# Two more unit pairs a layer by seven quarter products, and the first down operand split before the rest

## The chip, the cores and the metric

The kernel runs on one core of a Trainium2 chip. A core has a matrix engine (TensorE, in the profile PE, with its weight loads as PEld), a vector engine (DVE), a scalar engine (ACT), a general engine (POOL) and a queue that issues DMAs (SP). Matrix products are accumulated in eight PSUM banks; everything else lies in SBUF. The metric is the device time of one execution in microseconds (us), the median of three runs.

## The reference

Two decoder layers over 512 tokens of width 1024, all in float32. A layer has a mixing half (one wide input projection, a gated delta rule and a sliding-window attention, two up-projections, a merge and an output projection) and an MLP half. The change touches the MLP half alone:

```
h2 = rmsnorm(x, pre_mlp_g[l])                              # 512 x 1024
ff = jnp.square(jax.nn.relu(h2 @ w_ff1[l])) @ w_ff2[l]     # 1024 -> 4096 -> 1024
x = x + rmsnorm(ff, post_mlp_g[l])
```

## The kernel before

**Products of split operands.** Every float32 operand is split into a high part (`wh`, `h_h`, `P_h`; a cast by ACT) and a low part (`wl`, `h_l`, `P_l`; a subtraction by DVE). Each product of 128-row blocks is three matmuls: high by high, high by low, low by high.

**Weights.** They come packed in HBM, in pieces of 128 x 1024 float32 (512 KB), loaded by SP into raw buffers `wr` (six of them, `WR = 6`). `prefetch` casts a raw piece to `wh` (line 384, ACT) and subtracts to `wl` (line 385, DVE), into four buffers each (`LOOK = 4`). A call of `weights()` hands out the next prepared piece and prepares up to the third piece after it. So a piece is prepared early only as far as TensorE frees the buffers of the fourth piece before it.

**The MLP half.** The 4096 hidden columns are worked in four blocks, s = 0 to 3, of 1024. A block is an up part (eight units of 128 hidden columns for all 512 tokens) and a down part (1024 hidden columns times 1024 output columns).

- *A plain unit* (`mm_a`, lines 400 to 402) is 24 matmuls with 512 moving columns. Its bank is `ps_f1`, shown as `ps_f` in the profile. ACT takes relu and square from it (lines 1560, 1561 in `done`).
- *A pair of units* (`ff1`) is computed as a 2 x 2 product by seven quarter products in place of eight (Winograd's form). Each is 12 matmuls with 256 moving columns (`mm_h`, lines 473 to 476), so 84 a pair. The sums of activations (`n1` to `n4`) are made once a layer by `combos`, during block 0. The sums of weights are made for each pair by DVE in `up_specs` (line 343: four additions of 128 x 512). They need both raw units of the pair and two more raw buffers. A pair hands out four pieces: the two raw halves (first operand), two sums (second and third), and a half-wide tail (fourth). The intermediate results lie in banks `ps_a` (pool PM), `ps_y` (PZ), `ps_z` (PS) and `ps_q` (PK). The last two quarter products of a pair (`rest`) are issued after the first product of what follows.
- *The down part* of blocks 0 to 2 is also seven products, named after their left operands P1, P5, P6, P2, P7, P3, P4, each 24 matmuls with 512 columns (`mm_c`, lines 461 to 465). The left operands are quarters of the activated block and sums of them. They are made by `lefts` (seven splits and four vector additions, lines 1536 to 1542), once for each four units: `raw[0]` holds units 0 to 3, `raw[1]` holds 4 to 7, and `lefts` is called after the fourth and the eighth unit that is done. The right operands are sums of raw weights, made by DVE (`seven`, lines 304 and 309). Block 3 has a plain down part (`mm_b4`, `last_tiles`), and its activations are split directly (`h3`).
- When the block that follows begins with a pair, the second half of P4 is issued after that pair's first product (`split4`, `fourth`, `pending`).

**Which units are pairs** stands in `SEQ` (line 45), one entry a block: none in block 0; two in block 1, (4,5) and (2,3), between plain units 0, 1 and 6, 7; three in block 2, (0,1), (4,5), (2,3), then plain 6 and 7; four in block 3.

**The order of the work.** The framework fixes each engine's order at build time: earlier in the program has precedence, and an instruction whose inputs are ready can be put ahead of an earlier one that still waits. In `ff1` the order of TensorE is pinned as written (`Order`). On the other engines only the framework's order holds, and once built it is fixed: an instruction that waits holds up those behind it.

Of the kernel before, what the change touches and what calls it, by code (L numbers as in the profile page):

```python
# [41 lines left out]
WR = 6  # L42
FF_ORDER = (0, 4, 1, 5, 2, 6, 3, 7)
XB = 6
SEQ = (FF_ORDER, (0, 1, (4, 5), (2, 3), 6, 7), ((0, 1), (4, 5), (2, 3), 6, 7), ((0, 1), (2, 3), (4, 5), (6, 7)))

MIX = "G K K G K K G K K G K K G GA GA GA".split()
NA = sum(c.count("A") for c in MIX)
# [5 lines left out]
def units(seq):  # L54
    return [m for e in seq for m in (e if isinstance(e, tuple) else (e,))]
# [42 lines left out]
def chunk_keys(depth):  # L98

    keys = {}  # L100
    for kind, *key in chunk_order(depth):
        if kind == "chunk":
            keys[tuple(key)] = None
        elif kind == "up":
            l, s = key
            for m in units(SEQ[s]):
                keys["w_ff1", l, 0, (s * 8 + m) * P, 0] = None
# [20 lines left out]
def hybrid_trunk(ctx, tc, x, positions, pre_mix_g, dn_conv_w, dn_a_log, dn_dt_bias, dn_norm_g,  # L128
# [20 lines left out]
    def pool_of(tag, bufs):  # L149
        def get(name, dt=F32, n=512):  # L150
            return up.tile([P, n], dt, name=name, tag=tag, bufs=bufs)
        return get
# [5 lines left out]
    T = [pool_of(f"t{i}", 4) for i in range(9)]  # L158
# [14 lines left out]
    def PZ(name):  # L173
        return pp.tile([P, 512], F32, name=name, tag="ss", bufs=2)

    def PM(name):
        return pm.tile([P, 512], F32, name=name, tag="pm")
# [144 lines left out]
    def up_specs(l, s):  # L322
# [25 lines left out]
        last = None  # L348
        for n, e in enumerate(SEQ[s]):
            two = isinstance(e, tuple)  # L350
# [12 lines left out]
    for kind_, *key in chunk_order(depth):  # L363
        if kind_ == "seven":
            specs.extend(seven(*key))
        elif kind_ == "up":
            new = up_specs(*key)
            if isinstance(SEQ[key[1]][0], tuple):
                new.insert(1, specs.pop())
# [119 lines left out]
    def pair(U, name):  # L489
        return U(name + "_h", F32R), U(name + "_l", F32R)  # L490
# [104 lines left out]
    for l in range(depth):  # L595
# [859 lines left out]
        def ff1(done, rest=None):  # L1455
# [3 lines left out]
            order.begin()  # L1459
            for n, e in enumerate(SEQ[s]):  # L1460
                if not isinstance(e, tuple):
                    ps = PM("ps_f1")
                    w = weights()
                    if rest is None and not any(isinstance(x, tuple) for x in SEQ[s][n + 1:n + 2]):
                        mm_a(ps, h2, w=w)
# [55 lines left out]
        for s in range(3):  # L1521
            left = {f"P{i}": [] for i in range(1, 8)}
            later = {"P2": [], "P7": [], "P3": []}
            raw = [None, None]

            def make(name, T_, src, sign=1.0):
                p_ = pair(T_, name)
                split(src, *p_, sign)
                left[name].append(p_)

            def lefts(X, Y):

                a11, a21, a12, a22 = X[:, 0:512], X[:, 512:1024], Y[:, 0:512], Y[:, 512:1024]
                make("P1", T[5], a11)
                s1, s2 = T[4]("S1"), T[4]("S2")
                tt(out=s1, in0=a21, in1=a22, op=ALU.subtract)
                make("P5", T[7], s1)
                tt(out=s2, in0=a11, in1=s1, op=ALU.subtract)
                make("P6", T[1], s2)
                make("P4", T[2], a22, -1.0)  # L1540
                tt(out=s1, in0=a21, in1=a11, op=ALU.subtract)
                tt(out=s2, in0=a12, in1=s2, op=ALU.subtract)
                for name, src in (("P2", a12), ("P7", s1), ("P3", s2)):
                    later[name].append(src)

            def make_later(name, T_):
                for src in later[name]:
                    make(name, T_, src)

            count = [0]  # L1550

            def done(ms, ps):
                if len(ms) == 2:
                    raw[ms[0] // 4] = ps
                else:
                    m, = ms
                    if m in (0, 2, 4, 6):
                        raw[m // 4] = X4("raw")
                    r_ = raw[m // 4].rearrange("p (a k n) -> p a k n", a=2, k=2)[:, :, m % 2, :]
                    act(out=r_, in_=ps.rearrange("p (a n) -> p a n", a=2), func=AF.Relu)  # L1560
                    act(out=r_, in_=r_, func=AF.Square)
                count[0] += len(ms)
                if count[0] % 4 == 0:
                    lefts(*raw)

            if all(not isinstance(e, tuple) for e in SEQ[s]):
                for i, m in enumerate(SEQ[s]):
                    if s == 0 and i < 4:
                        ps = early[i][0]
                    else:  # L1570
                        ps = PM("ps_f1")
                        mm_a(ps, h2)
                    done((m,), ps)
                    if s == 0 and i in (1, 3, 5):
                        next(cg)
            else:
                ff1(done, pending)
            pa = [PZ("ps_pa") for t in range(2)]
            mm_c(pa, left["P1"])
            py = [PM("ps_py") for t in range(2)]  # L1580
            for t in range(2):
                act(out=py[t], in_=pa[t], func=AF.Copy, scale=-1.0)
            make_later("P2", T[5])
            pv = [PS("ps_pv") for t in range(2)]
            mm_c(pv, left["P5"])
            for t in range(2):
                into(2 + t, 1, pv[t])
            make_later("P7", T[7])
            pw_ = [PS("ps_pw"), PK("ps_pw")]
            for i, stale in enumerate((s == 0, any(isinstance(e, tuple) for e in SEQ[s]))):  # L1590
                if stale:
                    mm(pw_[i], lhsT=ones_r, rhs=h2[0][0], start=True, stop=True)
            mm_c(py, left["P6"], True)
            for t in range(2):
                nc.scalar.copy(pw_[t], py[t])
                into(t, 1, py[t])
            make_later("P3", T[1])
            mm_c(pa, left["P2"], True)
            for t in range(2):
                into(t, 0, pa[t])  # L1600
            mm_c(pw_, left["P7"], True)
            for t in range(2):
                tt(out=acc[2 + t][1], in0=pw_[t], in1=acc[2 + t][1], op=ALU.add)
            mm_c(pv, left["P3"], True)
            for t in range(2):
                tt(out=acc[t][1], in0=pv[t], in1=acc[t][1], op=ALU.add)

            def fourth(js, p_=left["P4"], pw_=pw_, s=s):
                mm_c(pw_, p_, True, js)
                if 1 not in js:  # L1610
                    return
                for t in range(2):
                    if s == 0:
                        act(out=acc[2 + t][0], in_=pw_[t], func=AF.Copy, scale=-1.0)
                    else:
                        tt(out=acc[2 + t][0], in0=acc[2 + t][0], in1=pw_[t], op=ALU.subtract)

            split4 = isinstance(SEQ[s + 1][0], tuple)
            fourth((0,) if split4 else range(2))
            pending = (lambda f=fourth: f((1,))) if split4 else None  # L1620
            if s == 0:
                next(cg, None)


        s = 3
# [54 lines left out]
```

## Time and profile before

| what | value |
|---|---|
| median of 3 runs | 1820.44 us (1819.75 to 1821.89) |
| the profiled execution | 1820.0 us, its span 1818.3 us |
| TensorE busy | 1796.3 us, 99% of the span, 10252 matmuls |
| weight loads busy | 1524.3 us, 84% |
| DVE busy | 1386.4 us, 76% |
| ACT busy | 994.9 us, 55% |
| granted TensorE clock | full speed in each of the 40 slices |

The profile is of one execution. "Busy" is the time in which an engine runs at least one instruction. A matmul is shown longer than the distance to the next, since matmuls overlap; what a stretch costs is read from start to start. The MLP half of layer 0 runs from about 581 to 912 us of the span, that of layer 1 from about 1481 to 1811 us. In layer 0 block 0's down part begins at 627.90, block 1 at 666.22, its down part at 708.20, block 2 at 743.79, its down part at 787.70, block 3 at 823.29 and its down part at 866.35.

### The profile page before, as it was taken

The page shows a single profiled execution, that of the slowest core. Times are in us where ns is not written, and L with a number is a line of the kernel's source. Part 1 is how long each engine was busy: PE and PEld are TensorE (multiplying, and loading weights), DVE is VectorE, ACT ScalarE, POOL GpSimd, SP SyncE. Part 2 cuts the span into 40 slices and gives each one's busy share as a digit, 9 for nine tenths or more (in the row PEclk, how much of TensorE's full clock was granted, in tenths as well). Part 3 has the DMA queues.
Part 4 walks back from the last instruction along what each step waited for, and adds up shares of the span by engine and source line. Part 5 has one row for each costly group of instructions (what it writes and reads, how often), then busy time and mean ns, then how long its engine had stood idle before and what let it go on. Part 6 is the DMA issues. An engine that isn't in the chain of part 4 may idle for free.

```text
span 1818.3 us, 28382 instructions
## 1 busy us (share of the span) xinstructions
PE 1796.3 (99%) x10252; PEld 1524.3 (84%) x10252; DVE 1386.4 (76%) x2606; ACT 994.9 (55%) x2031; POOL 209.4 (12%) x386
## 2 busy tenths in 40 slices
PE   9999999999999999999999999999999999999998
PEld 8878878888788888989898887888877888889896
DVE  5499796887666878898556997968875669798974
ACT  6678742444434656566457877234443347566562
POOL 0322102221101000000012221022111010000000
PEclk9999999999999999999999999999999999999999
DMA  6633447654463244554445344585545533554551
GB/s 201 203 111 121 111 145 226 180 170 152 117 200 136 82 162 153 174 182 146 166 155 180 105 128 110 168 230 157 166 140 153 172 116 105 175 166 158 174 176 57
DMA packets 146431, 278.60 MB, mean 153 GB/s; under 512 B 33569, under 2 KB 66657, under 8 KB 146290
## 3 DMA queue, kind: packets, MB, share of 16 engines
q1 hardware_dynamic: 145778, 276.75, 48.9%
q8 instruction: 81, 1.33, 0.3%
q14 instruction: 60, 0.49, 0.1%
q0 software_dynamic: 512, 0.03, 0.0%
HBM read 239.38 MB, written 37.36 MB: 152 GB/s over the span
## 4 chain that ended last, share of the span: by engine, by line
PE 82%; DVE 5%; ACT 5%; DMA 4%; issue 1%; POOL 1%; SPq 1%; DVEq 0%; POOLq 0%; ACTq 0%
PE ps_b L449 3%; PE ps_b L448 3%; PE ps_b L450 3%; PE ps_f L400 2%; PE ps_f L401 2%; PE ps_f L402 2%; PE ps_us L400 2%; PE ps_us L401 2%; PE ps_us L402 2%; PE ps_ud L401 2%; PE ps_ud L402 1%; PE ps_ud L400 1%; PE ps_vp L402 1%; PE ps_vp L400 1%; PE ps_vp L401 1%
## 5 line engine op out<-in xcount | busy, mean ns | idle before, releaser
L384 ACT CAST wh<-wr 128x1024 fp32r<-128x1024 f32 (+2 forms) x368 | 372.5, 1019 | 439.5 <-PE ps_vp L401 59.0
L385 DVE TENSOR_TENSOR wl<-wr,wh 128x1024 fp32r<-128x1024 f32 (+2 forms) x368 | 435.2, 1191 | 177.6 <-ACT wh L384 174.4
L512 POOL TENSOR_TENSOR pr<-pq,pw 128x1 f32<-128x1 f32 x16 | 9.8, 612 | 793.4 <-DVE pq L511 793.4
L448 PE MATMUL ps_b<-wh,h_h 128*128 128x432 f32 (+1 forms) x192 | 71.1, 370 | 0.0
L449 PE MATMUL ps_b<-wl,h_h 128*128 128x432 f32 (+1 forms) x192 | 70.5, 367 | 0.1
L450 PE MATMUL ps_b<-wh,h_l 128*128 128x432 f32 (+1 forms) x192 | 70.3, 366 | 0.0
L400 PE MATMUL ps_f<-g_h,wh 128*128 128x512 f32 x160 | 62.4, 390 | 0.0
L401 PE MATMUL ps_f<-g_l,wh 128*128 128x512 f32 x160 | 62.4, 390 | 0.0
L402 PE MATMUL ps_f<-g_h,wl 128*128 128x512 f32 x160 | 62.2, 389 | 0.0
L401 PE MATMUL ps_qp<-h_l,wh 128*128 128x512 f32 x128 | 54.0, 422 | 0.0
L400 PE MATMUL ps_vp<-h_h,wh 128*128 128x512 f32 x128 | 53.7, 420 | 0.0
L402 PE MATMUL ps_vp<-h_h,wl 128*128 128x512 f32 x128 | 53.7, 419 | 0.0
L985 ACT ACTIVATE M<-M,nm 128x128 f32<-128x128 f32 x128 | 49.9, 391 | 5.9 <-DVE nm L980 5.9
L400 PE MATMUL ps_qp<-h_h,wh 128*128 128x512 f32 x128 | 51.8, 405 | 0.0
L400 PE MATMUL ps_kp<-h_h,wh 128*128 128x512 f32 x128 | 51.6, 403 | 0.0
L402 PE MATMUL ps_qp<-h_h,wl 128*128 128x512 f32 x128 | 51.4, 401 | 0.0
L401 PE MATMUL ps_vp<-h_l,wh 128*128 128x512 f32 x128 | 51.4, 401 | 0.0
L401 PE MATMUL ps_ga<-h_l,wh 128*128 128x512 f32 x128 | 51.0, 398 | 0.0
L400 PE MATMUL ps_gb<-h_h,wh 128*128 128x512 f32 x128 | 51.0, 398 | 0.0
L402 PE MATMUL ps_kp<-h_h,wl 128*128 128x512 f32 x128 | 50.9, 398 | 0.0
L402 PE MATMUL ps_ga<-h_h,wl 128*128 128x512 f32 x128 | 50.7, 396 | 0.0
L343 DVE TENSOR_TENSOR wr<-wr 128x512 f32<-128x512 f32 x72 | 47.4, 685 | 4.3 <-DMA wr<-in_weights_dram 4.1
(432 smaller groups left out, 5922.5 us busy)
## 6 DMA issues: line engine op xcount, KB each, us to landing
wr<-in_weights_dram SPq DMA_DIRECT2D x320, 512.0 KB, 3.7
wr<-in_weights_dram SPq DMA_DIRECT2D x24, 432.0 KB, 4.7
D<-dd SPq DMA_DIRECT2D x32, 256.0 KB, 2.8
xd<-xo SPq DMA_DIRECT2D x12, 512.0 KB
xt<-xd SPq DMA_DIRECT2D x24, 256.0 KB, 4.1
D<-gd SPq DMA_DIRECT2D x16, 256.0 KB, 6.0
dd<-D SPq DMA_DIRECT2D x16, 256.0 KB, 5.9
kkd<-kk SPq DMA_DIRECT2D x16, 256.0 KB, 2.0
```

Of the source, the lines that this page charges most:

```text
L343: tt(out=o_, in0=i0, in1=i1, op=ALU.add)
L384: nc.scalar.copy(wh[:, :w], wr[:, :w])
L385: sub(out=wl[:, :w], in0=wr[:, :w], in1=wh[:, :w].bitcast(F32), op=ALU.subtract)
L400: mm(ps, lhsT=wh[:, k, :], rhs=hi, start=k == 0, stop=False)
L401: mm(ps, lhsT=wh[:, k, :], rhs=lo, start=False, stop=False)
L402: mm(ps, lhsT=wl[:, k, :], rhs=hi, start=False, stop=k == KT - 1)
L448: mm(pss[t], lhsT=hi[:, tsl], rhs=wh[:, r, :], start=k == 0, stop=False)
L449: mm(pss[t], lhsT=hi[:, tsl], rhs=wl[:, r, :], start=False, stop=False)
L450: mm(pss[t], lhsT=lo[:, tsl], rhs=wh[:, r, :], start=False, stop=k == KT - 1)
L512: ptt(out=r, in0=q1, in1=mhalf[:, 0:1], op=ALU.pow)
L985: act(out=M[:, j * P:(j + 1) * P], in_=M[:, j * P:(j + 1) * P], func=AF.Exp, bias=nm[:, j:j + 1], accum_out=den[:, j:j + 1])
```

## The change

`SEQ` now has three pairs in block 1, four in block 2 and four in block 3: eleven a layer, nine before. Block 1 takes the sequence that block 2 had, and block 2 that of block 3 with its middle pairs in another order. Block 1 now begins with a pair, so the second half of P4 of block 0 moves behind that pair's first product.

The left operand P1 of the first down product is no longer split in `lefts`. It is split in `done`, as soon as the first, and later the second, half of `raw[0]` is there (after unit 1 or pair (0,1), and after unit 3 or pair (2,3)).

In blocks 1 and 2 the banks of two down products change pools: `pa` (P1, then P2) takes PM, and `py` (P6) takes PZ. In block 0 they stay.

```
-SEQ = (FF_ORDER, (0, 1, (4, 5), (2, 3), 6, 7), ((0, 1), (4, 5), (2, 3), 6, 7), ((0, 1), (2, 3), (4, 5), (6, 7)))
+SEQ = (FF_ORDER, ((0, 1), (4, 5), (2, 3), 6, 7), ((0, 1), (4, 5), (2, 3), (6, 7)), ((0, 1), (2, 3), (4, 5), (6, 7)))
...
                 a11, a21, a12, a22 = X[:, 0:512], X[:, 512:1024], Y[:, 0:512], Y[:, 512:1024]
-                make("P1", T[5], a11)
                 s1, s2 = T[4]("S1"), T[4]("S2")
...
                 count[0] += len(ms)
+                if ms[-1] in (1, 3):
+                    make("P1", T[5], raw[0][:, 0:512])
                 if count[0] % 4 == 0:
                     lefts(*raw)
...
-            pa = [PZ("ps_pa") for t in range(2)]
+            pa = [(PM if s else PZ)("ps_pa") for t in range(2)]
             mm_c(pa, left["P1"])
-            py = [PM("ps_py") for t in range(2)]
+            py = [(PZ if s else PM)("ps_py") for t in range(2)]
```

## The prediction

> **What bounds the kernel now.** I read the page first, then busy time by stretch with the MLP half of layer 0 cut at its block borders, then the timelines of TensorE, DVE and ACT at the places that the change touches.
>
> ```profile
> span 1818.3 us, 28382 instructions
> PE 1796.3 (99%) x10252; PEld 1524.3 (84%) x10252; DVE 1386.4 (76%) x2606; ACT 994.9 (55%) x2031; POOL 209.4 (12%) x386
> PEclk9999999999999999999999999999999999999999
> PE 82%; DVE 5%; ACT 5%; DMA 4%; issue 1%; POOL 1%; SPq 1%; DVEq 0%; POOLq 0%; ACTq 0%
> L343 DVE TENSOR_TENSOR wr<-wr 128x512 f32<-128x512 f32 x72 | 47.4, 685 | 4.3 <-DMA wr<-in_weights_dram 4.1
> ```
>
> TensorE works 99% of the span at full granted clock, and 82% of the chain that ended last is TensorE. So matmul time that goes away shortens the run, as long as DVE, ACT and the loads still feed TensorE. The four weight additions of a pair (line 343: 72 are 4 in 9 pairs in 2 layers) are the only work of the up parts whose waits are on loads.
>
> ```profile
> core 0: us, PE busy (x) PEld busy (x) DVE busy (x) ACT busy (x) POOL busy (x), PEclk, DMA share, GB/s
> 627.90:666.22 38.32, 38.32 (x171) 31.72 (x170) 34.76 (x41) 26.17 (x37) 0.00 (x0) 1.00 0.60 200
> 666.22:708.20 41.98, 41.98 (x266) 38.16 (x265) 29.44 (x36) 24.16 (x39) 0.00 (x0) 1.00 0.44 138
> 708.20:743.79 35.59, 35.59 (x158) 29.46 (x157) 33.94 (x41) 20.24 (x27) 0.00 (x0) 1.00 0.50 161
> 743.79:787.70 43.91, 43.91 (x314) 41.49 (x313) 37.02 (x48) 28.00 (x45) 0.00 (x0) 1.00 0.52 169
> 787.70:823.29 35.59, 35.59 (x158) 29.47 (x157) 34.16 (x41) 20.32 (x27) 0.00 (x0) 1.00 0.50 162
> 823.29:866.35 43.06, 43.06 (x350) 42.56 (x348) 35.42 (x50) 30.12 (x50) 0.00 (x0) 1.00 0.53 160
> 1723.65:1767.37 43.72, 43.56 (x349) 42.66 (x348) 35.86 (x51) 30.21 (x50) 0.00 (x0) 1.00 0.50 159
> ```
>
> These are, in order: the down part of block 0, up and down of blocks 1 and 2, and up of block 3, all of layer 0; last, block 3 of layer 1. In layer 0 TensorE never pauses. In layer 1 the same block takes 0.66 us longer (43.72 against 43.06), the only loss there is. DVE is close behind TensorE: 33.94 of 35.59 us in a down part (95%), 37.02 of 43.91 in block 2 (84%).
>
> **The change part by part.** *The pairs.* Pace, from start to start:
>
> ```profile
> 787.70 0.39 PE L461 MATMUL ps_pa<-wh,P_h 128*128 128x512 f32 x1
> 789.05 0.39 PE L461 MATMUL ps_pa<-wh,P_h 128*128 128x512 f32 x1
> ...
> 847.63 0.28 PE L473 MATMUL ps_y<-n_h,wh 128*128 128x256 f32 x1
> 849.07 0.28 PE L473 MATMUL ps_a<-g_h,wh 128*128 128x256 f32 x1
> ```
>
> Six matmuls of 512 columns lie between the first two starts, twelve of 256 between the last two: 1.44 / 12 = 0.120 us for the narrow. For the wide the down part is the finer ruler: 157 matmuls (thirteen pieces of 12, and a filler) in 35.59 us, 0.2267 each. Two plain units are 48 x 0.2267 = 10.88 us, a pair 84 x 0.120 = 10.08. Saved: 0.80 us a pair, not the eighth (1.36) that the arithmetic promises. Check: block 1 is four plain units and two pairs, 21.76 + 20.16 = 41.92, measured 41.98. Block 1 gains a pair and block 2 gains one, in two layers: 4 x 0.80 = **-3.2 us**, 0.18%.
>
> The Trainium skill (TensorE: Matmul & The Clock Gate, section Back-to-back issue gap) gives a warm gap of N / 2.4 + 2.5 ns, so 215.8 and 109.2 ns; by that an estimate of a pair's saving is 1.19 us and of the whole 4.7 us. The trace does not agree: 226.7 and 120 ns here, and the nine pairs that exist already run at that pace. I go by the trace.
>
> *What a pair asks of DVE and ACT.*
>
> ```profile
> 731.04 2.36 DVE L385 TENSOR_TENSOR wl<-wr,wh 128x1024 fp32r<-128x1024 f32 x2
> 846.62 1.29 DVE L343 TENSOR_TENSOR wr<-wr 128x512 f32<-128x512 f32 x2
> L1506 DVE SCALAR_TENSOR_TENSOR raw<-ps_z,raw x18: 416/420/425, 684.6 to 1764.8; 128x256 f32<-128x256 f32 x18
> L1510 DVE TENSOR_TENSOR raw<-ps_y,raw x18: 417/424/425, 687.4 to 1766.8; 128x256 f32<-128x256 f32 x18
> ```
>
> Queued one behind the other, a full subtraction takes about 1.18 us (2.36 / 2) and a half-wide operation 0.65 (1.29 / 2). A pair needs three and a half subtractions, four additions and the two short ones: 3 x 1.18 + 0.65 + 4 x 0.65 + 2 x 0.42 = 7.6 us. Two plain units need 2.4. So DVE gets +5.2 us a pair, 10.4 a layer. From 627.90 to 866.35 DVE is busy 34.76 + 29.44 + 33.94 + 37.02 + 34.16 + 35.42 = 204.7 of 238.5 us (86%); after, 215 of 237 (91%). It still fits as a whole. ACT has room (28.00 of 43.91 in block 2). The number and size of loads stay; a pair only holds four of six raw buffers at once.
>
> *Block 1* gets the sequence of block 2 before, after a down part with less DVE work for its length (34.76 of 38.32 against 33.94 of 35.59). That sequence ran without a pause after the harder one (41.12 + 2.72 for the half of P4 = 43.84 of 43.91). Cost 0, bounds 0 to 0.5 a layer. The moved half of P4 costs its own 12 matmuls, as before.
>
> *Block 2* is where I expect the loss. Its DVE time becomes 37.02 + 5.2 = 42.2 of 43.1 us, 98%. The place is the seven operations of `lefts` in the third pair:
>
> ```profile
> 770.71 0.69 DVE L1536 TENSOR_TENSOR S<-raw 128x512 f32<-128x512 f32 x1
> 774.46 0.68 DVE L1542 TENSOR_TENSOR S<-raw,S 128x512 f32<-128x512 f32 x1
> 775.06 1.82 DVE L385 TENSOR_TENSOR wl<-wr,wh 128x512 fp32r<-128x512 f32 x2
> ...
> 778.07 0.28 PE L473 MATMUL ps_z<-n_h,wh 128*128 128x256 f32 x1
> ```
>
> They hold DVE from 770.71 to 775.06 (4.35 us); then come the third pair's tail and the low part of unit 7 (to 776.88). TensorE needs the tail at 778.07. With a fourth pair in place of units 6 and 7, a quarter product (1.44) stands where half a unit stood (2.72). The tail is needed at 776.8, one us after it is ready, and the fourth pair's second operand at 776.8 + 1.44 = 778.2. If the fourth pair's additions are done before `lefts`, the second operand is ready at about 776.9: no loss. If they come after it (1.3), then the cast (1.05) and the subtraction (1.22), it is ready at 775.7 + 3.6 = 779.3: 1.1 us late, and the third operand, with 3.6 more against 2.9 of TensorE work, another 0.7. Bounds 0 to 1.8 a layer. Block 3 before, also four pairs, does the additions early (846.62 above, in its third pair), and loses 0 in layer 0 and 0.66 in layer 1. I take the mean of these, **0.35** a layer.
>
> *Down part of block 2.* The 98% leave DVE late at its start, by what its waits add. Before, DVE stood still 6.9 us in block 2 (43.91 - 37.02). If half of these waits stay, it is 42.2 + 3.4 - 43.1 = 2.5 us late. Against that stand 1.43 us of idle in the down part (35.59 - 34.16) and the spare of its tightest piece:
>
> ```profile
> 732.91 0.39 PE L461 MATMUL ps_pw<-wh,P_h 128*128 128x512 f32 x1
> ```
>
> The low part that this matmul needs is the first of the two at 731.04, done at 732.26: 0.65 us to spare, and block 2's down part has the same schedule. So 2.1 us are free and 0.4 remain. Bounds 0 to 1.3; I take **0.25** a layer, as `lefts` also starts sooner after a pair than after a plain unit.
>
> *The banks.* In block 1 `pa` now follows units 6 and 7 in pool PM:
>
> ```profile
> 787.67 1.05 ACT L384 CAST wh<-wr 128x1024 fp32r<-128x1024 f32 x1 [2.99 <-PE ps_f L401]
> 788.62 0.59 ACT L1560 ACTIVATE raw<-ps_f 128x512 f32<-128x512 f32 x1
> ```
>
> This is block 2 before, the same order. Unit 7's bank is read until 789.21, and the second half of P1 would start at 789.05, so it waits 0.2 us, unless the rest of the first half goes ahead. Bounds 0 to 0.2, I take **0.1** a layer. Behind the waiting matmul stands only TensorE's own queue. `py` in PZ finds banks read long before: 0.
>
> *P1 split early* moves two casts and two subtractions a block and adds none. In block 1 and 2 they come where DVE has waits; without the move, the last pair of block 2 would be followed by square, cast and subtraction before P1's second half, 2.7 us against the same 2.7 of its first half: 0, bounds 0 to 0.3.
>
> **Sum:** -3.2 + 2 x (0.35 + 0.25 + 0.1) = -1.8 us. The profiled execution took 1820.0 (span 1818.3 and 1.7 around it), so 1818.2; the median lies 0.4 above that execution: **1818.6**.
>
> **The rivals.** *All of it arrives.* DVE's waits absorb everything, and the loss in layer 1's block 3 may go too: -3.2 to -3.9, so 1816.6 to 1817.2. For it: 86% becomes only 91%, and layer 0 has no pause now. Against: 98% in block 2.
>
> *DVE takes it all.* The fourth pair's additions come after `lefts` in both layers: 2 x (1.8 + 0.1 + a late start of the down part, 0.25 or more) = 4.3, net +1.1, about 1821.5. For it: precedence, since `lefts` is earlier in the program. Against: the early additions in block 3.
>
> *Slower: a late load with DVE's queue behind it.*
>
> ```profile
> 844.88 0.69 DVE L343 TENSOR_TENSOR wr<-wr 128x512 f32<-128x512 f32 x1 [0.87 <-DMA wr<-in_weights_dram]
> ...
> 1746.21 0.69 DVE L343 TENSOR_TENSOR wr<-wr 128x512 f32<-128x512 f32 x1 [1.85 <-DMA wr<-in_weights_dram]
> 1746.82 1.22 DVE L385 TENSOR_TENSOR wl<-wr,wh 128x1024 fp32r<-128x1024 f32 x1
> ```
>
> In block 3 the fourth pair's first addition waits for its raw unit, whose load waits for a raw buffer that an earlier subtraction frees; the subtraction that TensorE needs next stands behind it. In layer 1 the wait is 0.98 us longer than in layer 0, and TensorE loses 0.66: about 0.3 us is free. If in block 2 `lefts` (4.35) goes ahead of the subtraction that frees the buffer, the load goes out 4.35 later and TensorE loses 4.0 a layer: -1.8 - 0.7 + 8.0 = +5.5, 1826. It decides from 2.0 us of delay a layer on (1.6 of gain, 0.3 free). Against: before, `lefts` starts only after the next operand's subtraction (770.71). The Trainium skill (Perfetto Trace Analysis, section Tensor Engine Instruction) calls the queues of DVE and ACT strict first in, first out; the trace agrees, as 1746.82 follows right on 1746.21.
>
> **How the numbers follow.** Forecast 0.60, all arrives 0.17, DVE takes it 0.15, late load 0.08. A measurement of this kernel tells about 0.2% (3.6 us) from no change, so *faster* means below 1816.8: the upper half of the second case, 0.07. *Slower* means above 1824.1: the late load, 0.07. *Same* is the rest, 0.86. The range takes in the second and third case: 1816.7 to 1822.0.
>
> **What would show it.** TensorE has 10252 + 4 x 36 = 10396 matmuls, and line 343 counts 88. Block 1's stretch is 0.8 shorter, block 2's 0.1 to 0.8. A pause of TensorE before `ps_y` or `ps_q` in the fourth pair of block 2 shows the second term, one before `ps_pw` the third, one within `ps_pa` of block 1 the fourth. DVE is above 95% in block 2. I am wrong if pairs run at another pace than 0.120 us, if a pause stands elsewhere in the MLP half, or if the time leaves the range.

## The result and the profile after

The changed kernel takes 1825.11 us (median of 21 runs, 1823.1 to 1831.04), the kernel before 1822.17 in the runs beside it (21 runs, 1817.87 to 1825.08). The ratio is 1.0020, 95% interval 1.0013 to 1.0027: **3.6 us slower** (2.4 to 4.9). The ratio is taken over all runs; the two medians differ by 2.9 us. The forecast was 1.8 us faster, and the time lies above its range; 1.7 us of that distance is the kernel before itself, which took 1820.44 in the three runs that the forecast starts from. The profiled execution took 1826.3.

First the page of the changed kernel: the span, the busy times, the granted clock, the chain that ended last by engine, and two groups.

```profile
span 1824.6 us, 28730 instructions
PE 1796.2 (98%) x10396; PEld 1530.1 (84%) x10396; DVE 1405.2 (77%) x2638; ACT 1006.3 (55%) x2051; POOL 211.6 (12%) x386
PEclk9999999999999999999999999999999999999999
PE 79%; DVE 8%; DMA 5%; ACT 5%; issue 2%; POOL 1%; SPq 0%; DVEq 0%; POOLq 0%; ACTq 0%
L343 DVE TENSOR_TENSOR wr<-wr 128x512 f32<-128x512 f32 x88 | 57.7, 686 | 5.7 <-DMA wr<-in_weights_dram 5.5
L473 PE MATMUL ps_z<-n_h,wh 128*128 128x256 f32 x176 | 50.2, 285 | 3.7 <-DVE raw L1506 3.7
```

The change is there: 10396 matmuls, 88 weight additions. Yet TensorE's busy time is as before (1796.2 us against 1796.3), its share of the chain fell from 82% to 79%, and DVE's rose from 5% to 8%. The last row names the place: TensorE stood 3.7 us before `ps_z`, and what ended that was line 1506, DVE's read of `ps_z`. No such row was on the page before.

Busy time by stretch of the changed kernel: layer 1's down part of block 0, up and down of blocks 1 and 2, and up of block 3, in this order; then block 2's up part in layer 0. The columns are those shown for the kernel before.

```profile
1533.53:1569.13 35.60, 35.60 (x158) 29.48 (x157) 33.44 (x39) 23.59 (x34) 0.00 (x0) 1.00 0.59 189
1569.13:1613.03 43.90, 43.90 (x313) 41.49 (x312) 35.76 (x46) 29.00 (x47) 0.00 (x0) 1.00 0.50 157
1613.03:1648.73 35.70, 35.70 (x158) 29.40 (x157) 34.12 (x41) 20.48 (x27) 0.00 (x0) 1.00 0.50 161
1648.73:1693.58 44.85, 43.27 (x350) 42.60 (x349) 38.51 (x54) 30.11 (x49) 0.00 (x0) 1.00 0.48 148
1693.58:1729.46 35.88, 35.88 (x160) 29.32 (x158) 35.88 (x43) 21.08 (x28) 0.00 (x0) 1.00 0.56 172
1729.46:1773.69 44.23, 43.30 (x350) 42.61 (x348) 36.68 (x51) 30.20 (x50) 0.00 (x0) 1.00 0.52 163
...
741.87:788.34 46.47, 44.25 (x349) 42.81 (x348) 39.68 (x55) 29.93 (x49) 0.00 (x0) 1.00 0.48 150
```

Each stretch has a length that it would have without a pause, by the paces of the prediction: a down part 35.60, block 1 (three pairs, two units, half of P4) 43.84, a block of four pairs and half of P4 4 x 10.08 + 2.72 = 43.04. Against these, block 1 loses 0.06, its down part 0.10, **block 2 1.81** (3.43 in layer 0), its down part 0.28, and **block 3 1.19**. In the down part of block 2 DVE is busy 35.88 of 35.88 us: it never rests. Within block 2 it is busy only 38.51 of 44.85 us (86%).

The span of the profiled execution is 6.3 us longer than that of the kernel before. From block 0's down part to the last product of block 3 the two layers take 287.33 and 283.48 us (283.97 and 282.44 before), which is 4.4 of the 6.3. The rest lies outside these stretches. There, in the mixing half of layer 1, a pause of 1.9 us was followed by 3.5 us at a granted clock of 0.51 (1377.0 to 1380.5), which the profile before does not have.

The waits of TensorE in layer 1's MLP half of the changed kernel (engine, what it was about to do, what it waited for; total, times, longest) hold two entries in the blocks, where the kernel before has none. This view counts from the modelled end of the matmul before and so shows some 0.15 us less than the distance of the starts.

```profile
PE ps_z L473 <- DVE raw L1506: 1.6, 1, 1.6
PE ps_y L476 <- DVE wl L385: 0.9, 1, 0.9
```

The first is in block 2. DVE and TensorE there, the changed kernel:

```profile
1676.79 0.69 DVE L1535 TENSOR_TENSOR S<-raw 128x512 f32<-128x512 f32 x1
...
1680.53 0.69 DVE L1541 TENSOR_TENSOR S<-raw,S 128x512 f32<-128x512 f32 x1
1681.14 1.82 DVE L385 TENSOR_TENSOR wl<-wr,wh 128x512 fp32r<-128x512 f32 x2
1682.87 0.42 DVE L1506 SCALAR_TENSOR_TENSOR raw<-ps_z,raw 128x256 f32<-128x256 f32 x1
...
1683.44 0.35 PE L473 MATMUL ps_z<-n_h,wh 128*128 128x256 f32 x1 [1.58 <-DVE raw L1506]
```

And the same place of the kernel before (its TensorE row at 778.07 is in the prediction):

```profile
776.79 0.42 DVE L1506 SCALAR_TENSOR_TENSOR raw<-ps_z,raw 128x256 f32<-128x256 f32 x1
```

The third pair's tail is accumulated into `ps_z`, and before that DVE must have read what stands in it (line 1506). DVE does its seven operations of `lefts` first (1676.79 to 1681.14; the rows between are left out), then two subtractions, then the read. Before, TensorE came 0.86 us after that read was done (778.07 - 777.21), because half a plain unit (2.72) lay between. Now a quarter product (1.44) lies there, and TensorE starts 1.73 us later than its pace would allow. The weights were not what it waited for: the tail's are the first of the two subtractions at 1681.14, done about 0.7 later, at 1681.8. Without the pause TensorE would have started at 1683.44 - 1.73 = 1681.71, and the first matmul that reads this low part (line 476) is its third.

The second is at the start of block 3, in the changed kernel:

```profile
1730.17 1.89 DVE L343 TENSOR_TENSOR wr<-wr 128x512 f32<-128x512 f32 x3
1732.48 0.69 DVE L1617 TENSOR_TENSOR acc<-acc,ps_pw 128x512 f32<-128x512 f32 x1 [0.42 <-PE ps_pw L465]
1733.08 0.69 DVE L343 TENSOR_TENSOR wr<-wr 128x512 f32<-128x512 f32 x1
1733.69 1.22 DVE L385 TENSOR_TENSOR wl<-wr,wh 128x1024 fp32r<-128x1024 f32 x1
...
1734.96 0.39 PE L476 MATMUL ps_y<-n_h,wl 128*128 128x256 f32 x1 [0.93 <-DVE wl L385]
```

And the start of block 3 in the kernel before, layer 0, where the block begins at 823.29 (line 1616 there is line 1617 of the changed kernel):

```profile
820.94 0.68 DVE L343 TENSOR_TENSOR wr<-wr 128x512 f32<-128x512 f32 x1
...
825.24 2.48 DVE L385 TENSOR_TENSOR wl<-wr,wh 128x1024 fp32r<-128x1024 f32 x2
827.63 1.28 DVE L1616 TENSOR_TENSOR acc<-acc,ps_pw 128x512 f32<-128x512 f32 x2
```

Before, the first of the first pair's sums was made 2.35 us ahead of the block. In the changed kernel the sums begin only 0.71 us after the block did (1730.17 against 1729.46). The second operand's `wl` then stands behind line 1617, which itself waits 0.42 us for `ps_pw`; before, two `wl` subtractions (825.24) stood ahead of that line.

### The profile page after: what moved, and what is told of

Its sections match the earlier page's. It is cut to its first block, busy times and chain, and to the rows that moved or that the text cites. A ratio compares the mean times of both kernels' runs of the same rounds, so it can differ in the third digit from the quotient of the medians.

```text
span 1824.6 us, 28730 instructions
## 1 busy us (share of the span) xinstructions
PE 1796.2 (98%) x10396; PEld 1530.1 (84%) x10396; DVE 1405.2 (77%) x2638; ACT 1006.3 (55%) x2051; POOL 211.6 (12%) x386
## 4 chain that ended last, share of the span: by engine, by line
PE 79%; DVE 8%; DMA 5%; ACT 5%; issue 2%; POOL 1%; SPq 0%; DVEq 0%; POOLq 0%; ACTq 0%
PE ps_b L449 3%; PE ps_b L448 3%; PE ps_b L450 3%; DVE wl L385 2%; DMA wr<-in_weights_dram 2%; PE ps_us L400 2%; PE ps_us L402 2%; PE ps_us L401 2%; PE ps_vp L400 2%; PE ps_vp L402 2%; PE ps_ud L401 2%; PE ps_ud L402 1%; PE ps_ud L400 1%; PE ps_vp L401 1%; PE ps_qp L400 1%
## 5 line engine op out<-in xcount | busy, mean ns | idle before, releaser
L384 ACT CAST wh<-wr 128x1024 fp32r<-128x1024 f32 (+2 forms) x376 | 378.8, 1015 | 421.6 <-PE ps_us L401 60.2
L385 DVE TENSOR_TENSOR wl<-wr,wh 128x1024 fp32r<-128x1024 f32 (+2 forms) x376 | 442.3, 1186 | 160.6 <-ACT wh L384 157.2
L343 DVE TENSOR_TENSOR wr<-wr 128x512 f32<-128x512 f32 x88 | 57.7, 686 | 5.7 <-DMA wr<-in_weights_dram 5.5
L473 PE MATMUL ps_z<-n_h,wh 128*128 128x256 f32 x176 | 50.2, 285 | 3.7 <-DVE raw L1506 3.7
L400 PE MATMUL ps_ga<-h_h,wh 128*128 128x512 f32 x128 | 50.8, 397 | 0.0
L401 PE MATMUL ps_gb<-h_l,wh 128*128 128x512 f32 x128 | 50.6, 395 | 0.0
```

The lines of the kernel that those rows point to most:

```text
L343: tt(out=o_, in0=i0, in1=i1, op=ALU.add)
L384: nc.scalar.copy(wh[:, :w], wr[:, :w])
L385: sub(out=wl[:, :w], in0=wr[:, :w], in1=wh[:, :w].bitcast(F32), op=ALU.subtract)
L400: mm(ps, lhsT=wh[:, k, :], rhs=hi, start=k == 0, stop=False)
L401: mm(ps, lhsT=wh[:, k, :], rhs=lo, start=False, stop=False)
L473: mm(ps, lhsT=wh[:, k0 + k, :], rhs=hi, start=start and k == 0, stop=False, skip_group_check=True)
```

## The experiments

All are timed in five rounds beside the kernel before on the same chip. Two theories run through them. *Order:* DVE's work fits, only single operations stand in the wrong place of its queue. *Load:* DVE has too much to do in block 2 and the down part behind it, and what is freed in one place comes back in another.

**One block alone.** Block 1's pair without block 2's, and the reverse; the other edits stay.

```
e2  SEQ blocks 1, 2, 3: 3, 3, 4 pairs     ((0, 1), (4, 5), (2, 3), 6, 7) twice
e3  SEQ blocks 1, 2, 3: 2, 4, 4 pairs     (0, 1, (4, 5), (2, 3), 6, 7), ((0, 1), (4, 5), (2, 3), (6, 7))
```

> Three pairs in block 1, three in block 2 as before, four in block 3; P1 split early and banks swapped as in the change. Order theory (the loss comes from the seven operations of lefts standing on DVE ahead of the read of ps_z at line 1506 when a fourth pair follows, and from what that leaves late): no fourth pair in block 2, so no pause before ps_z, block 2 43.9 us, its down part 35.7, block 3 43.1 to 43.7; gain 2 x 0.8 less 2 x 2 x 0.09 for the banks: 1.2 us faster than before. DVE theory (DVE has no room for the 5.2 us of any further pair, wherever it stands): a third pair in block 1 leaves pauses of 0.8 or more in block 1 or its down part, 0 to 2 us slower than before.

> Two pairs in block 1 as before, four in block 2, four in block 3; the other edits as in the change. Order theory: block 2 pauses 1.8 us before ps_z of the third pair's tail, its down part 0.3, block 3 1.2, as in the changed kernel, 2.6 us a layer slower on balance: 5 us slower than before. DVE theory: with one pair less in block 1 DVE has 5 us more room a layer, and the pauses shrink to half or less: 0 to 2 us slower than before.

Measured: 3, 3, 4 pairs 1817.19 against 1817.7, ratio 0.9995 (0.9987 to 1.0004); 2, 4, 4 pairs 1823.83, ratio 1.0029 (1.0019 to 1.0039). The loss comes with block 2's fourth pair; block 1's third costs nothing that can be told in time. The first run's profile does lose 0.77 us at the start of layer 1's block 1, where TensorE waits before `ps_y` for a copy by ACT (line 1487) that stands behind two casts; the changed kernel's profile does not. In the second run's layer 1 TensorE waits 1.8 us before `ps_z` for line 1506 and 0.9 before `ps_y` for `wl`: the same two as in the changed kernel, so they need no change in block 1.

**The left operands later.** The first `lefts` of a block that begins with pairs is called after the third pair's line 1506. DVE's work is the same.

```
-                if count[0] % 4 == 0:
+                if count[0] == 4 and len(ms) == 2:
+                    late.append(lambda X=raw[0], Y=raw[1]: lefts(X, Y))
+                elif count[0] % 4 == 0:
                     lefts(*raw)
...
                 stt(out=R[:, half(3)], in0=z, scalar=-1.0, in1=q_, op0=ALU.mult, op1=ALU.subtract)
+                while late:
+                    late.pop()()
```

> The changed kernel, but the first lefts of a block that begins with a pair is called after the third pair's line 1506, so that this read of ps_z has precedence. DVE's work is the same. Order theory: the pause of 1.8 us before ps_z goes, block 2 is about 43.1 us; its down part (35.9) and block 3 (44.2) stay as they are; 3.6 us faster than the changed kernel, level with before. DVE theory: TensorE reaches the down part 1.8 us earlier while DVE is no earlier, so the same 1.8 us comes back in the down part of block 2 and in block 3: no faster than the changed kernel.

Measured: 1818.8 against 1817.7, ratio 1.0005 (0.9997 to 1.0014), some 2.7 us below the changed kernel by the two ratios. Its DVE timeline, and its TensorE waits in layer 1:

```profile
1672.96 1.28 DVE L487 TENSOR_TENSOR P_l<-S,P_h 128x512 fp32r<-128x512 f32 x2
1674.17 0.41 DVE L1506 SCALAR_TENSOR_TENSOR raw<-ps_z,raw 128x256 f32<-128x256 f32 x1
...
1682.86 1.22 DVE L304 TENSOR_TENSOR wr<-wr 128x1024 f32<-128x1024 f32 x1
1684.00 0.42 DVE L1506 SCALAR_TENSOR_TENSOR raw<-ps_z,raw 128x256 f32<-128x256 f32 x1
```

```profile
PE ps_y L476 <- DVE wl L385: 0.9, 1, 0.9
PE ps_z L473 <- DVE raw L1506: 0.4, 1, 0.4
```

The framework still put five of the seven ahead, but the third pair's read now comes in time and its pause is gone. With the same work on DVE this is the order theory's result for the first pause. Not all came back: now the fourth pair's read (1684.00) stands behind a weight sum and is 0.52 us late by the starts, and block 3's pause is untouched.

**The additions of `lefts` on POOL.**

```
-                tt(out=s1, in0=a21, in1=a22, op=ALU.subtract)
+                ptt(out=s1, in0=a21, in1=a22, op=ALU.subtract)      # and the other three alike; ptt is tt on POOL
```

> The changed kernel with the four vector additions of lefts on POOL: DVE is freed of 2.4 us at each lefts, 4.8 us a block in blocks 0 to 2; POOL took 1.28 us for an operation of this size. Order theory: the read of ps_z comes 2.4 us sooner, its pause goes (1.8 us a layer); what is left is at most 0.3 and 1.2. DVE theory: all pauses go, block 2 43.1, its down part 35.6, block 3 43.1, and the whole gain of 3.2 us less 0.4 for the banks arrives: 2.8 us faster than before. If the slower chain on POOL decides, a pause stands before ps_pv or ps_py in the down parts.

Measured, in four runs: 1847.49, ratio 1.0162 (1.0149 to 1.0175), 29 us slower than the kernel before. POOL, then DVE, in layer 1's first down part:

```profile
1544.61 1.52 POOL L1535 TENSOR_TENSOR S<-raw 128x512 f32<-128x512 f32 x1 [15.15 <-ACT raw L1560]
1546.21 2.16 POOL L1537 TENSOR_TENSOR S<-raw,S 128x512 f32<-128x512 f32 x1
```

```profile
1544.90 2.32 DVE L385 TENSOR_TENSOR wl<-wr,wh 128x1024 fp32r<-128x1024 f32 x1
1547.25 2.20 DVE L304 TENSOR_TENSOR wr<-wr 128x1024 f32<-128x1024 f32 x1
1549.37 0.68 DVE L487 TENSOR_TENSOR P_l<-S,P_h 128x512 fp32r<-128x512 f32 x1
```

A subtraction that takes 1.2 us elsewhere takes 2.32 here, a sum 2.20; the next one, with POOL at rest from 1548.37 on, takes its usual 0.68. The numbers fit two engines that take turns: POOL's first ends at 1546.13, 1.09 before DVE's subtraction ends (1547.22); POOL's second ends at 1548.37, 1.08 before DVE's sum does (1549.45). The Trainium skill (SBUF — State Buffer, section Who interferes with whom) says that a DVE instruction with two SBUF inputs and a GpSimd one that reads SBUF exclude each other for the whole instruction; the trace agrees. So an operation of 0.69 us that DVE is spared can come back as a wait of up to 1.1 us for POOL's. POOL also takes 1.5 to 2.2 us for what DVE did in 0.69, so left operands come later (in this down part TensorE waits 1.1 us before `ps_pv` for one). How much of the 29 us is the one and how much the other was not separated.

**ACT reads `ps_z`.** The copy that frees `ps_z` goes to ACT in all pairs, and DVE subtracts in SBUF afterwards.

```
-                stt(out=R[:, half(3)], in0=z, scalar=-1.0, in1=q_, op0=ALU.mult, op1=ALU.subtract)
+                act(out=R[:, half(3)], in_=z, func=AF.Copy, scale=-1.0)
+                tt(out=R[:, half(3)], in0=R[:, half(3)], in1=q_, op=ALU.subtract)
```

> The changed kernel, but the read of ps_z that the third and every other pair's tail waits for is made by ACT (a 128x256 copy with scale -1 into the raw tile), and DVE subtracts ps_q's copy in SBUF afterwards; DVE's number of operations stays the same, and its order is left to the framework. Order theory (the pause in block 2 is the tail waiting for a read that stands behind seven operations of the left operands in DVE's queue): the 1.73 to 1.94 us at that place go, in layer 0 also the smaller ones before ps_z, in all 3.6 to 4.2 us below the changed kernel; what is left is 1.4 us a layer (block 3's second operand 1.19, down part 0.11, banks 0.09) against a gain of 1.6, so level with the kernel before, within 1 us. Load theory (DVE simply has too much to do in block 2 and its end): the pause turns up at the next wl or at ps_y's read instead, and the kernel stays 2.5 to 4 us above the kernel before.

Measured: 1820.74 against 1817.72, ratio 1.0016 (1.0008 to 1.0025). The new ones among its TensorE waits in layer 1, and its down part of block 2:

```profile
PE ps_pv L461 <- ACT wh L384: 0.2, 1, 0.2
PE ps_py L463 <- DVE wl L385: 0.2, 1, 0.2
```

```profile
1685.81:1722.43 36.62, 36.26 (x159) 29.25 (x158) 36.62 (x45) 20.90 (x28) 0.00 (x0) 1.00 0.55 174
```

In layer 1 the pause before `ps_z` is gone, as the order theory said, but the time is what the load theory said: two new waits in the down part, which is now 1.02 us longer than 35.60, with DVE at work in all of it. Block 3's 0.9 stays. TensorE comes sooner to a DVE that is no sooner done. There is a rival to that reading: one of the new waits is for ACT's cast, and ACT has the extra copies. Both waits return in e7 and e13 below, which keep ACT's read, and neither is above 0.2 us in e4 and e14, which take the same pause away by order alone. Load and ACT's copies are not separated by this run.

**The order at the start of block 3**, alone (e9) and with ACT's read (e7): `behind` adds an order without a wait between two DVE instructions. (In the rows of these two and of e12 and e14 line 393 is the `wl` subtraction, 347 a pair's sum.)

```
                     tt(out=o_, in0=i0, in1=i1, op=ALU.add)
+                    if s == 3 and ms[0] == 0 and n_ == "b":
+                        behind(b["end"])                # the second operand's last sum
...
                         tt(out=acc[2 + t][0], in0=acc[2 + t][0], in1=pw_[t], op=ALU.subtract)
+                        if s == 2:
+                            behind(subs[used[0]])       # the second operand's wl
```

> The changed kernel with two orders fixed on DVE at the start of block 3 alone: the sums of the first pair's second operand are made before any of its third operand, and the two subtractions of ps_pw into acc (line 1617 of the changed kernel) stand behind the second operand's wl. No operation is added or removed. Order theory: wl is 0.6 us earlier through the sums and 1.1 us through the subtractions (0.42 of waiting for ps_pw and 0.69), so the 1.19 us before ps_y's second operand go in both layers: 2.4 us below the changed kernel, about 1.2 above the kernel before, and block 2's 1.73 to 1.94 stay. Load theory: what is put behind is late itself, and the pause moves to the copy into ps_z or to ps_q's wl: no more than 0.5 us below the changed kernel, about 3 above the kernel before.

> Both of them: ACT reads ps_z, and the order at the start of block 3. If the two pauses are separate and are all that the change loses, the sum holds: 3.6 and 2.4 us below the changed kernel, about 2.4 us below the kernel before, near the 3.2 us that four more pairs save less 0.2 a layer. If DVE is full in the down part before block 3, the pause comes back in another place and it stays within 0.5 us of e6.

Measured: alone 1820.89, ratio 1.0022 (1.0013 to 1.0031), which is the changed kernel's; both 1819.12, ratio 1.0006 (0.9997 to 1.0014). Alone, DVE and ACT at that place:

```profile
1727.02 2.61 DVE L347 TENSOR_TENSOR wr<-wr 128x512 f32<-128x512 f32 x4
1729.60 1.23 DVE L393 TENSOR_TENSOR wl<-wr,wh 128x1024 fp32r<-128x1024 f32 x1
```

```profile
1728.52 1.05 ACT L392 CAST wh<-wr 128x1024 fp32r<-128x1024 f32 x1 [0.82 <-DVE wr L347]
```

The order is as wished, and the pause shrinks from 1.09 to 0.75 us only: the sums begin at 1727.02, 1.31 after the block's start (1725.71), the cast at 1728.52, and `wl` cannot come before it. What is late is DVE as a whole, out of the down part (argued from these rows here; e11 tests it). My expectation of 2.4 us was wrong, and that of e7, 2.4 us below the kernel before, with it.

**Less load.** The six additions into `acc` of line 1407 are left out in the down part of block 2, in the changed kernel (e11) and in e7 (e12).

```
-            else:
+            elif s == 1:
                 tt(out=acc[t][n], in0=ps, in1=acc[t][n], op=ALU.add)
```

> The changed kernel without the six additions of 128x512 into acc that line 1407 makes in the down part of block 2 (ps_pv, ps_py, ps_pa; the output lacks that part of block 2): 4.1 us of DVE's work less in 35.9 us in which DVE never rests. Load theory (DVE enters block 3 late because the down part before it is full): the 1.19 us before block 3's second operand and the 0.11 to 0.28 in the down part go in both layers, 2.6 us below the changed kernel, about 1 us above the kernel before; block 2's 1.73 to 1.94 us stay. Order theory (block 3's pause is the order at its start alone: the wait of 0.42 us for ps_pw at the head of the queue and the subtraction ahead of wl): it goes no further down than the run that fixed this order, 0.7 us below the changed kernel, about 3 us above the kernel before.

> Both orders fixed (ACT reads ps_z, order at the start of block 3) and the same six additions left out. In the run with both orders the pauses left in and behind the down part of block 2 are 0.67 before ps_py, 0.49 before ps_pv and 0.28 to 0.41 in block 3, 1.5 us a layer. Load theory: they go with DVE's load, about 3 us below the run with both orders, 2 us below the kernel before: the 3.2 us of four more pairs come out but for the banks and some small pauses in block 2. Rival (these pauses are set by ACT's casts, which the copy of ps_z delays, or by the weights' loads): they stay, within 0.8 us of the run with both orders, 0.5 to 1.5 us above the kernel before.

Measured: 1822.22 against 1817.81, ratio 1.0023 (1.0014 to 1.0033); and 1818.64, ratio 1.0004 (0.9995 to 1.0013). In time neither came down as I had expected. In the profile, e11's block 3 in layer 1 starts without the pause: the distance before `ps_y` there is 0.1 us over the pace, and the down part takes 35.69 with DVE busy 33.03. So that pause is DVE's lateness out of a full down part, though leaving work out also let the framework make the first sum earlier, and the two are not separated. Two other things took the gain: a late load in layer 0's block 3 (1.01 us before `ps_y`; in layer 1 a late `wl`, 0.65), and a slower TensorE clock after block 2's pause in layer 1. DVE in layer 0, and two stretches of block 2 in layer 1 around and behind that pause:

```profile
846.90 0.69 DVE L343 TENSOR_TENSOR wr<-wr 128x512 f32<-128x512 f32 x1 [2.54 <-DMA wr<-in_weights_dram]
```

```profile
1676.00:1677.50 1.50, 0.00 (x0) 0.00 (x0) 1.50 (x3) 0.93 (x1) 0.00 (x0) 1.00 0.43 52
1677.70:1681.20 3.50, 3.45 (x17) 3.48 (x18) 1.70 (x3) 1.43 (x3) 0.00 (x0) 0.53 0.87 300
```

e12 has the least pauses of the runs with eleven pairs. Most of what is left is before `ps_py`; in layer 1:

```profile
PE ps_py L472 <- DVE wl L393: 0.3, 1, 0.3
```

**The other edits alone, and 3, 3, 4 pairs in other forms.** e1: the kernel before with the early split and the banks. e8: the kernel before with 3, 3, 4 pairs alone. e10: 3, 3, 4 pairs, early split, old banks, ACT's read.

> The kernel before with the two edits that are no pairs: P1's split right behind the first operand, and ps_pa and ps_py in each other's banks in blocks 1 and 2; pairs 2, 3 and 4. The early split moves two operations on DVE and two on ACT and adds none: 0. The banks: 0.09 us in each of up to four down parts, as in the changed kernel's trace before ps_pa. So 0 to 0.4 us above the kernel before. If the early split is what spares the run of 3, 3 and 4 pairs with both edits some wait (it came out 0.0013 below the one without them), it is 0.5 to 1.5 us below the kernel before.

> The kernel before with block 1's order of units alone changed to three pairs and two single units (3, 3 and 4 pairs); P1's split stays in the left operands and the accumulators stay in their banks. Against the earlier run of 3, 3 and 4 pairs with the other two edits it lacks the 0.09 us a down part before ps_pa: 0.36 us faster than that run, 0.9 us below the kernel before. If the early split of P1 was worth something, it is slower than that run instead: within 0.3 us of the kernel before or above it.

> 3, 3 and 4 pairs with the early split of P1, the banks as in the kernel before, and ACT reading ps_z. Two more pairs in all: 1.6 us less; no 0.09 us for the banks; no wait of a tail for DVE (0.42 in the earlier run); left are 0.67 us or so before block 1's ps_y in one layer. Order theory: 1.0 to 1.8 us below the kernel before. Load theory (ACT's eleven copies a layer hold up the casts of the weights): the pauses of the run with ACT's read and four pairs (0.65 before ps_py, 0.50 before ps_pv in a down part) come back here too, and it is level with the kernel before.

Measured: e1 1818.3 against 1817.81, ratio 1.0005 (0.9997 to 1.0014); e8 1818.65 against 1817.72, 1.0008 (0.9999 to 1.0017); e10 1818.41 against 1817.81, 1.0003 (0.9995 to 1.0012). All level. e1's profile has no pause in its blocks but the banks' 0.09 in each of four down parts and one of 0.08. e8's trace has late loads in block 3 (1.9 us of pauses in layer 0, 0.6 in layer 1) that the earlier run of 3, 3, 4 pairs did not have, and 1.03 us in layer 1's block 1 for the same copy by ACT as in e2; whether the late loads are the missing early split or chance, one profile each does not tell.

**The orders together.** e4's later `lefts` and block 3's order (e14), and with ACT's read in block 2's fourth pair alone (e13).

```
+                if s == 2 and n == 3:
+                    act(out=R[:, half(3)], in_=z, func=AF.Copy, scale=-1.0)
+                    tt(out=R[:, half(3)], in0=R[:, half(3)], in1=q_, op=ALU.subtract)
+                else:
                     stt(out=R[:, half(3)], in0=z, scalar=-1.0, in1=q_, op0=ALU.mult, op1=ALU.subtract)
```

> The changed kernel with the first left operands behind the third pair's read of ps_z (as in the earlier run that put them later), the order at the start of block 3 fixed, and ACT reading ps_z in block 2's fourth pair alone. If the three pauses are separate, a layer keeps 0.09 before ps_pa, 0.11 in the down part and 0.2 to 0.4 in block 3, so that the profile shows about 0.7 us of pauses a layer where no load is late, and the time is 1.5 to 2.5 us below the kernel before. If pauses come back wherever DVE is behind (as in the runs with ACT's reads in all pairs: 0.65 before ps_py, 0.49 before ps_pv), it is within 1 us of the kernel before.

> The same without ACT's read of ps_z in the fourth pair: there DVE's read stays 0.52 to 0.72 us late, as in the run with the left operands later. Separate pauses: 0.6 us a layer above the run with all three, 0.3 to 1.3 us below the kernel before. Pauses that come back: level with it.

Measured: both 0.9997 (0.9988 to 1.0006), 1818.51 and 1818.06 against 1818.67. That is 4 us better than the changed kernel and level with the kernel before. Block 2, its down part and block 3 of e14 in layer 1:

```profile
1643.06:1687.01 43.95, 43.40 (x350) 42.67 (x348) 38.45 (x54) 29.81 (x49) 0.00 (x0) 1.00 0.48 151
1687.01:1722.91 35.90, 35.90 (x160) 29.32 (x158) 35.90 (x43) 21.10 (x28) 0.00 (x0) 1.00 0.57 173
1722.91:1766.23 43.32, 43.31 (x349) 42.61 (x348) 36.73 (x51) 30.26 (x50) 0.00 (x0) 1.00 0.55 169
```

0.91 + 0.30 + 0.28 us lost, against 1.6 gained; in e13 0.58 to 0.77 is back before block 3's `ps_y`. So order takes away some 4 us of what the changed kernel loses, but the whole 3.2 us of gain came out in none of the orders tried. No version tried beats the kernel before by more than the measurement tells.

**One sum over all of them.** For each kernel I added up the pauses of TensorE in the MLP halves of its one profile (distances of starts over the pace by more than 0.06 us), took 0.7 for the pauses of the kernel before's profile, and 0.8 a pair added.

| kernel | pairs added | pauses, us | pauses - 0.7 - 0.8 a pair | measured difference to before, us |
|---|---|---|---|---|
| changed | 4 | 8.1 | +4.2 | +3.6 (2.4 to 4.9) |
| e1 split and banks | 0 | 0.5 | -0.2 | +0.9 (-0.5 to 2.5) |
| e2 3, 3, 4 | 2 | 1.7 | -0.6 | -0.9 (-2.4 to 0.7) |
| e3 2, 4, 4 | 2 | 7.1 | +4.8 | +5.3 (3.5 to 7.1) |
| e4 lefts later | 4 | 6.1 | +2.2 | +0.9 (-0.5 to 2.5) |
| e5 POOL | 4 | 32.7 | +28.8 | +29.4 (27.1 to 31.8) |
| e6 ACT's read | 4 | 6.5 | +2.7 | +2.9 (1.5 to 4.5) |
| e7 both orders | 4 | 5.0 | +1.1 | +1.1 (-0.5 to 2.5) |
| e8 3, 3, 4 alone | 2 | 4.0 | +1.7 | +1.5 (-0.2 to 3.1) |
| e9 block 3's order | 4 | 7.5 | +3.6 | +4.0 (2.4 to 5.6) |
| e10 3, 3, 4, ACT's read | 2 | 2.0 | -0.3 | +0.5 (-0.9 to 2.2) |
| e11 no additions | 4 | 8.7 | +4.8 | +4.2 (2.5 to 6.0) |
| e12 both orders, no additions | 4 | 3.0 | -0.9 | +0.7 (-0.9 to 2.4) |
| e13 three orders | 4 | 5.0 | +1.1 | -0.5 (-2.2 to 1.1) |
| e14 two orders | 4 | 3.7 | -0.1 | -0.5 (-2.2 to 1.1) |

The sum lies within or at the edge of the interval each time. The intervals are some 3 us wide, so the profiles test the gain of a pair more sharply. The stretches from block 0's down part to the last product of block 3 (283.97 and 282.44 before, 287.33 and 283.48 changed) hold 0.18 and 0.68 us of such pauses before, and 5.02 and 3.20 in the changed kernel. Without them each layer is 1.48 us shorter, 0.74 a pair. So 0.80 us a pair holds within 0.06, and the time of each kernel is that gain less its pauses in the MLP half, as far as the intervals tell.

## Why the prediction was wrong, point by point

- *The gain*, 0.80 a pair and -3.2 in all: right, by the matmul count, by block 1 (43.90 against 43.84 by the paces), and by the stretches above (0.74 a pair).
- *Block 1*, 0: right in the changed kernel's profile (0.06), and e2 shows no loss in time. But layer 1's block 1 lost 0.77 us in e2's profile and 1.03 in e8's, over the bound of 0.5, so some of this is luck of the execution. *The early split*, 0: e1 is level, and its profile shows no pause for it. *The banks*, 0.1 a layer: right, 0.09 to 0.10 in block 1's down part.
- *Block 2*, 0.35 a layer, bounds 0 to 1.8: **the step that failed.** "The tail is needed at 776.8, one us after it is ready" looked at the tail's weights alone. The tail also needs DVE to have read `ps_z`, and that read began at 776.79 before, the very time at which I put the need. It came to 1.81 us in layer 1 and 3.43 in layer 0, where another 0.46 before `ps_z` and late `wl` come on top. The working of the prediction shows line 1506 and prices its 0.42 us of DVE, not its place in the queue. What I looked at instead went as the better case said: the fourth pair's additions are made before `lefts`.
- *The down part of block 2*, 0.25: right in size, 0.28. The pause that was to show it, before `ps_pw`, did not come; there is one of 0.11 before `ps_pv`, and the rest is in steps too small to place.
- *Block 3*: **left out.** I let DVE's lateness end with the down part ("2.1 us are free and 0.4 remain"). DVE worked 35.88 of 35.88 us there, so nothing was made up, and block 3's first sums came late: 1.19 us in layer 1, with a pause of the same size in layer 0.
- *DVE's 98% in block 2*: wrong. It was 86% (38.51 of 44.85), since DVE waits there too. The work that did not fit between its waits slid into the down part (34.16 to 35.88) and block 3 (35.42 to 36.68), counted against layer 0 before.
- *The signs*: block 1's stretch did not become 0.8 shorter, because it now holds the moved half of P4; without these 2.72 us it is 41.18, which is 0.80 less than 41.98. Block 2's grew.
- *The sum* with the measured terms of layer 1 in both layers: -3.2 + 2 x (1.81 + 0.28 + 0.10 + 0.06 + 1.19) = +3.7 us; measured +3.6. That it comes so close is partly luck: it leaves out what layer 0 lost beyond layer 1, and the 0.7 us of pauses that the kernel before has itself. With both, the table's +4.2 is the fairer figure.
- *The rivals*: "all of it arrives" is out. "DVE takes it all" had the right engine and the wrong operations. "A late load" plays a part in some profiles (e8, e11), not in the two pauses that both layers of the changed kernel have.

What stays open: e4 shows that order makes the first pause, e11 that a less loaded DVE does away with the second. How much of what remained in e7 and e13 is load, how much ACT's copies and how much the framework's choice was not separated: in e12 0.53 us before `ps_py` remained in layer 1 with 4.1 us less work for DVE, which came later in the queue than that `wl`.

## What to carry to other kernels

When TensorE's work between two points shrinks, check every reason for which the instruction behind it may start, not only its weights: a bank that is accumulated into again must have been read, and the place of that read in its engine's queue counts, not its length. Here DVE was 95% busy in the down part before the change, and lateness that came into it was handed on to block 3; so price the stages behind the one that gets more work. A pause that is taken away is worth only what the rest lets through: with ACT's read 3.7 us of waits before `ps_z` went and 0.7 us of time came, while order alone, at both places, brought 4.

## What the hardware showed that was not expected

Two-input operations of POOL and DVE take turns, in whole instructions (rows above): 1.2 us became 2.2 to 2.35.

The granted TensorE clock fell to about half after some pauses of about two us, for about 3.5 us. In e5, behind two pauses of 1.2 and 2.3 us:

```profile
643.00:645.00 2.00, 1.85 (x5) 1.52 (x6) 2.00 (x4) 0.00 (x0) 0.00 (x0) 0.64 0.55 215
645.00:647.00 2.00, 2.00 (x6) 1.52 (x6) 1.57 (x2) 1.07 (x2) 0.00 (x0) 0.50 0.74 240
```

The starts are 0.427 us apart there, in place of 0.2267, which cost 1.7 us beside the pause itself; in e11 it cost 1.6 behind a pause of 1.95 (block 2 of layer 1, clock 0.53). Pauses of 1.7 to 1.9 us at the same place in both layers of the changed kernel and in layer 0 of e11 cost no clock, and neither did two of 2.3 us in e5. The Trainium skill (TensorE: Matmul & The Clock Gate, section What's actually happening) tells of a free-running window of about 3.4 us, after which an idle TensorE is set to half clock and a busy one to full. The 3.5 us and the half agree, and a window that runs free would explain why one pause of 1.9 us is hit and another is not; that TensorE need not idle for a whole window is what the runs show beyond it.
